# Eight column pairs by eleven block products instead of seven, the residual kept in memory meanwhile, and fixed places for the preparation steps of the last part

## The chip, the cores and the metric

The kernel runs on one core of one Trainium2 chip. The metric is device time in microseconds. TensorE does the matmuls (weights are loaded beside them), VectorE and ScalarE the elementwise work, GpSimd issues transfers and does a little arithmetic, SyncE (SP) issues most loads. Each engine takes its instructions in the order in which they were issued to it.

## The reference

One step of a two-layer model on 384 rows: 256 of a prompt and 8 × 16 of samples, so three blocks of 128 rows. D = 2048, C = 4096, everything float32. Layer 0 (attention of two kinds) comes first and is not touched by the change. Layer 1 and the end are:

```python
h = rmsnorm(x, norm1_g)                       # x: residual, 384 x 2048
p = einsum('bsd,dn->bsn', h, w_in1)           # w_in1: 2048 x 12288
u, v, z = p[..., :C], layernorm(p[..., C:2*C], ln_g, ln_b), p[..., 2*C:]
w = where(causal, w_sp, 0)                    # 16 groups of 256 columns, chunks of 128 rows
mixed = einsum('gts,bnsgc->bntgc', w, v) + b_sp
x = x + einsum('bsn,nd->bsd', u * mixed * silu(z), w_out1)     # w_out1: 4096 x 2048
y = rmsnorm(x, final_g)
```

The normalised v rows of the samples are an output too.

## The kernel before, in words

**Three products for each matmul.** Every float32 operand is split into a high part (a rounded copy, by ScalarE) and a low part (what is left, by VectorE), and each product is made as high·high, high·low and low·high (`products`, lines 100 to 102). A weight block of 128 × 512 is loaded by SP (`raw`), copied by ScalarE (`whi`, line 84) and subtracted by VectorE (`wlo`, line 86). `dense_nat` does this for a column of 512: for each of `KT` = 16 row blocks of the weights, nine matmuls, three for each block of rows of the activations, so 144 for a column with 2048 input rows. After every two row blocks it may call a step of other work, a hook (`between`).

**A pair of columns by fewer products.** Two columns can be made together by `seven`, which forms sums of the weights' and of the activations' quarters as fast matrix multiplication does: the first two blocks of 128 rows take seven block products for eight, the third takes its four as usual. That makes eleven block products of 24 matmuls, 264, where two columns by `dense_nat` take 288. `seven` has three phases of four steps each, `singles`, `chain` and `pair`; a step loads one to four wide blocks (128 × 1024, line 932, tile `sraw`), may add or subtract them on VectorE (`add`, line 958), splits them (`split2`, lines 90 and 91, tiles `shi` and `slo`) and multiplies (`stream`, lines 945 to 947, into banks `a`). The sums of the activations are made once, by `token_sums`, inside the second dense column (`sumh`, `suml`). `wide()` gives the wide buffers, five of them; `shi` and `slo` have three each.

**Order in the middle of layer 1.** Two columns of v come from `dense_nat`, the other six from three pairs (`v_pair`). Then z column c and u column c come together from one `zu_pair`, for c below `NP`; the columns from `NP` to 6 are made by `eight`, as in `dense_nat`, and their single row blocks are laid in between the steps of the pairs by the numbers in `mix`: how many ordinary row blocks stand ahead of each of the four steps of `chain` and of `pair`. `run` prepares each step (loads, sums, splits) before the products of the step ahead of it are issued. z is passed through Silu and multiplied with u and `rstd`, and the result, the gate, goes to memory (`gd`); v goes to memory too (`vd`).

**The last part.** Column 7 of z and of u come from two `dense_nat` calls; z's Silu is line 1239, u's multiplication line 1242. Their hooks, and those of `out1`, carry `prepare(c)` for c = 0 to 7: load v and the gate and the spatial weights (small loads on GpSimd's queue, line 1173), normalise v, split it, do the spatial matmuls (lines 1209 to 1211) and multiply the gate by the result (line 1213); then `turn` the gate (VectorE transposes 32 × 32 squares, line 132, and sixteen GpSimd transfers move them to their places in `gTt`, line 135) and split the turned gate into two slots (lines 1221 and 1222). `hooked(c)` runs c's steps and then c + 1's, one step a hook. `out1(k0, 8)` multiplies eight row blocks of `w_out1` with the gates of two values of c, for each of four output columns, and adds the result to the residual `h1`, which lies in four slots on the chip (line 1166). It is called for row blocks 0, 8 and 16; a shorter last part closes the sums and normalises. TensorE's dense results go to banks `d`; a column takes three, and there are four.

Of the kernel before, what the change touches and what calls it, by code (L numbers as in the profile page):

```python
# [15 lines left out]
P = 128  # L16
DM = 2048
KT = DM // P
NT = 3
# [13 lines left out]
def f32(ap):  # L33
    return ap.bitcast(F32)
# [3 lines left out]
def tile_hybrid_step(  # L38
# [828 lines left out]
    with ExitStack() as l1:  # L867
# [8 lines left out]
        with ExitStack() as lv:  # L876
# [25 lines left out]
                    gated(z, tb, o[tb])  # L902
                G.dma_start(gd[c], z)

            sums_hi, sums_lo = [], []

            def wide():
                return vp.tile([P, 2, 512], F32, tag="sraw", bufs=5, name=nm("sraw"))

            def token_sums(q):  # L910

                hi, lo = h1c[q]
                full, t = wide().rearrange("p j (h t) -> p j h t", h=2), wide().rearrange("p j (h t) -> p (j h) t", h=2).rearrange("p i (j t) -> p i j t", j=2)
                V.tensor_tensor(out=full.rearrange("p j h t -> p (j h) t"), in0=f32(hi[:, :, :2 * P]), in1=f32(lo[:, :, :2 * P]), op=ALU.add)
                a11, a12, a21, a22 = (full[:, :, h, tb * P:tb * P + P] for tb in range(2) for h in range(2))
                for i, (x, y) in enumerate(((a21, a22), (a11, t[:, 0]), (a21, a11), (a12, t[:, 1]))):
                    V.tensor_tensor(out=t[:, i], in0=x, in1=y, op=ALU.subtract)
                th, tl = (vp.tile([P, 4, 2, P], F32R, tag=tag, bufs=4, name=nm(tag)) for tag in ("sumh", "suml"))
                split(th, tl, t)
                sums_hi.append(th)  # L920
                sums_lo.append(tl)

            def row(tb, half):
                return lambda k: [x[2 * k + half][:, tb * P:(tb + 1) * P] for x in (hh_, hl_)]

            def tsum(i):
                return lambda k: [x[k // 2][:, i, k % 2, :] for x in (sums_hi, sums_lo)]

            def load2(u, half, c0):

# [2 lines left out]
                return raw  # L933

            def split2(raw):
                hi, lo = (vp.tile([P, 2 * WPITCH], F32R, tag=tag, bufs=3, name=nm(tag))[:, :1024].rearrange("p (j c) -> p j c", j=2) for tag in ("shi", "slo"))
                split(hi, lo, raw)
                return hi, lo

# [144 lines left out]
            for make, c in [(v_pair, c) for c in (2, 4, 6)] + [(zu_pair, c) for c in range(NP)]:  # L1084
                p = []

                def part(i, make=make, c=c, p=p):
                    def f(u):
                        if not p:
                            p.extend(make(c))  # L1090
                        return p[i][0](u) if u is not None else p[i][1]()
                    return f

                def closing(i, part=part):
                    f = part(i)
# [145 lines left out]
        for tb in range(NT):  # L1241
            V.scalar_tensor_tensor(out=z7[:, tb, :], in0=o[tb], scalar=rstd[:, tb:tb + 1], in1=z7[:, tb, :], op0=ALU.mult, op1=ALU.mult)
        G.dma_start(gd[7], z7)
        for k0 in (0, 8, 16):
            if k0 == 16:
                for j in range(2):
# [121 lines left out]
```

## Time and profile before

| | |
|---|---|
| time, median of 3 runs | 1789.45 us (1788.18 to 1797.57) |
| profiled execution: its time / its span | 1793.24 us / 1791.5 us |
| mean granted TensorE clock | 0.993 |
| layer 0 and the two dense columns of v | 0 to 780 us |
| pairs of v | 780 to 1046 us |
| pairs of z and u, with the ordinary row blocks among them | 1046 to 1425.8 us |
| u column 7 and the start of the last part ("the seam") | 1425.8 to 1500 us |
| three calls of `out1` | 1500 to 1760 us |

A row of a stage lists busy time of each engine in it. The rows of the trace give the start, the duration, the engine, the line of the kernel, the operation and its tiles; brackets hold the idle time of that engine just before, and what ended it. Names of tiles stand without their numbers there.

### The profile page before, as it was taken

To read this page: it belongs to the slowest core of one execution; us is meant where nothing else is said; L and a number is where in the kernel's file an instruction comes from. 1 tells how busy PE (TensorE), PEld (TensorE's weight loads), DVE (VectorE), ACT (ScalarE), POOL (GpSimd) and SP (SyncE) were. 2 spreads that over 40 slices of the span, in tenths; PEclk is the share of its full clock that TensorE was granted. 3 is DMA by queue.
4 is the path that set the end of the run, shared out by engine and by line. 5 is a ranking of instruction groups with operands and counts; after the bars stand their busy time and mean duration, and the time that the engine had idled before them with its cause. 6 is when DMAs were issued, how large, how long until landed. Compare 5 with 4: busy or idle time off the path is not lost. (4 is left out here: it accounts for less than half of the span.)

```text
span 1791.5 us, 24294 instructions
## 1 busy us (share of the span) xinstructions
PE 1748.9 (98%) x8395; PEld 1443.9 (81%) x8395; DVE 1203.1 (67%) x1784; ACT 787.5 (44%) x1273; POOL 407.2 (23%) x621
## 2 busy tenths in 40 slices
PE   9999999999999999999999999999999969999998
PEld 8987888888888888888888887787777758877887
DVE  6347475457457455677697877777777767787766
ACT  5435353345337344444454435344444334334334
POOL 6426543223221110100200000000000154455220
PEclk9999999999999999999999999999999989999999
DMA  8789989778868876677777777777776677677653
GB/s 226 195 220 199 278 214 236 221 183 226 232 177 219 252 178 168 176 266 233 249 255 264 235 258 222 232 251 238 224 224 222 200 215 235 201 207 219 190 146 116
DMA packets 218028, 389.83 MB, mean 218 GB/s; under 512 B 24024, under 2 KB 62480, under 8 KB 217904
## 3 DMA queue, kind: packets, MB, share of 16 engines
q1 hardware_dynamic: 156368, 284.09, 52.9%
q0 software_dynamic: 30704, 88.05, 19.0%
q10 hardware_dynamic: 30832, 16.13, 3.1%
q8 instruction: 66, 1.08, 0.3%
q14 instruction: 58, 0.48, 0.1%
HBM read 339.87 MB, written 42.00 MB: 213 GB/s over the span
## 5 line engine op out<-in xcount | busy, mean ns | idle before, releaser
L101 PE MATMUL d<-wlo,slot 128*128 128x512 f32 x1677 | 652.2, 390 | 0.0
L102 PE MATMUL d<-whi,slot 128*128 128x512 f32 x1677 | 650.7, 390 | 0.0
L100 PE MATMUL d<-whi,slot 128*128 128x512 f32 x1677 | 608.4, 391 | 15.6 <-ACT slot L1239 15.6
L86 DVE TENSOR_TENSOR wlo<-raw,whi 128x512 fp32r<-128x512 f32 x546 | 374.7, 696 | 313.0 <-ACT whi L84 311.0
L84 ACT ACTIVATE whi<-raw 128x512 fp32r<-128x512 f32 x546 | 342.3, 630 | 525.9 <-PE d L102 448.1
L100 PEld LDWEIGHTS d<-whi,slot 128*128 128x128 f32 x1677 | 315.3, 188 | 84.1 <-ACT slot L1239 16.1
L102 PEld LDWEIGHTS d<-whi,slot 128*128 128x128 f32 x1677 | 315.3, 188 | 66.0
L101 PEld LDWEIGHTS d<-wlo,slot 128*128 128x128 f32 x1677 | 315.4, 188 | 65.0 <-DVE wlo L86 0.2
L90 ACT ACTIVATE shi<-sraw 128x1024 fp32r<-128x1024 f32 x196 | 208.0, 1061 | 272.4 <-PE a L947 228.5
L91 DVE TENSOR_TENSOR slo<-sraw,shi 128x1024 fp32r<-128x1024 f32 x196 | 236.4, 1218 | 36.8 <-ACT shi L90 35.7
L958 DVE TENSOR_TENSOR sraw<-sraw,sraw 128x1024 f32<-128x1024 f32 x112 | 136.9, 1222 | 110.8 <-DMA sraw<-in_w_in_dram 104.0
L946 PE MATMUL a<-slo,slot 128*128 128x512 f32 x392 | 153.2, 391 | 3.3 <-DVE slo L91 3.2
L947 PE MATMUL a<-shi,slot 128*128 128x512 f32 x392 | 152.6, 389 | 0.0
L945 PE MATMUL a<-shi,slot 128*128 128x512 f32 x392 | 147.1, 390 | 0.0
L135 POOL DMA_DIRECT2D gTt<-trn x128 | 78.3, 619 | 97.1 <-ACT whi L84 69.7
L946 PE MATMUL a<-slo,sumh 128*128 128x512 f32 x224 | 89.1, 398 | 8.3 <-DVE slo L91 8.2
L946 PEld LDWEIGHTS a<-slo,slot 128*128 128x128 f32 x392 | 73.7, 188 | 20.6 <-DVE slo L91 5.4
L945 PE MATMUL a<-shi,sumh 128*128 128x512 f32 x224 | 87.9, 392 | 2.2 <-DVE slot L958 2.2
L947 PE MATMUL a<-shi,suml 128*128 128x512 f32 x224 | 88.0, 393 | 0.0
L945 PEld LDWEIGHTS a<-shi,slot 128*128 128x128 f32 x392 | 73.7, 188 | 15.4
L947 PEld LDWEIGHTS a<-shi,slot 128*128 128x128 f32 x392 | 73.7, 188 | 15.2
L464 POOL DMA_DIRECT2D slot<-d x48 | 44.1, 926 | 128.2 <-DVE wlo L86 52.7
(307 smaller groups left out, 1704.6 us busy)
## 6 DMA issues: line engine op xcount, KB each, us to landing
sraw<-in_w_in_dram SPq DMA_DIRECT2D x224, 512.0 KB, 4.6
raw<-in_w_in_dram SPq DMA_DIRECT2D x416, 256.0 KB, 4.4
raw<-in_w_out_dram SPq DMA_DIRECT2D x175, 256.0 KB, 4.1
slot<-d POOLq DMA_DIRECT2D x48, 192.0 KB, 6.2
d<-slot ACTq DMA_DIRECT2D x24, 256.0 KB, 4.2
vd<-slot POOLq DMA_DIRECT2D x8, 768.0 KB, 6.3
gd<-slot POOLq DMA_DIRECT2D x8, 768.0 KB, 6.1
v<-vd POOLq DMA_DIRECT2D x8, 768.0 KB, 7.0
```

Source lines behind the costliest of these rows:

```text
L84: highs.append(S.activation(hi, raw, AF.Copy).ins)
L86: splits.append(V.tensor_tensor(out=lo, in0=raw, in1=f32(hi), op=ALU.subtract).ins)
L90: S.activation(hi_out, src, AF.Copy)
L91: V.tensor_tensor(out=lo_out, in0=src, in1=f32(hi_out), op=ALU.subtract)
L100: PE.matmul(o, lhsT=his[k][:, t], rhs=hi[:, 0, :], start=(k == first), stop=False)
L101: PE.matmul(o, lhsT=his[k][:, t], rhs=lo[:, 0, :], start=False, stop=False)
L102: mm = PE.matmul(o, lhsT=los[k][:, t], rhs=hi[:, 0, :], start=False, stop=(k == last))
L135: G.dma_start(dst[32 * j:32 * j + 32, :, 32 * a:32 * a + 32], trn[32 * a:32 * a + 32, :, 32 * j:32 * j + 32])
L945: PE.matmul(o, lhsT=xh, rhs=hi[:, j, :], start=(u + j == 0), stop=False)
L946: PE.matmul(o, lhsT=xh, rhs=lo[:, j, :], start=False, stop=False)
L947: PE.matmul(o, lhsT=xl, rhs=hi[:, j, :], start=False, stop=(u == 3 and j == 1))
L958: V.tensor_tensor(out=out, in0=x, in1=y, op=op)
```

## The change

Five pairs of z and u are made by `seven` instead of four (`NP`), so four ordinary columns are left instead of six, and `mix` lays in fewer of their row blocks. `wide()` has eight buffers, `shi` and `slo` four. The high parts of the token sums, and the low parts of two of the four, go into shared slots, which are free because the residual is not kept in its four slots during this time: it is loaded back from `h1d`, where it lies in memory anyway, by twelve GpSimd transfers after u's column 7. In the last part the steps of `prepare` get fixed places (`first_plan`, `later_plan`): each hook runs the steps that the plan lists for it, for c and c + 1 side by side. `prepare` loads its two normalising vectors (`lg`, now two buffers) ahead of the gate, and has one more step, between the turn and the two split operations.

```diff
-                return vp.tile([P, 2, 512], F32, tag="sraw", bufs=5, name=nm("sraw"))
+                return vp.tile([P, 2, 512], F32, tag="sraw", bufs=8, name=nm("sraw"))
...
-                th, tl = (vp.tile([P, 4, 2, P], F32R, tag=tag, bufs=4, name=nm(tag)) for tag in ("sumh", "suml"))
-                split(th, tl, t)
...
+                x = slot().rearrange("p (i j t) -> p i j t", j=2, t=P)
+                th = x[:, :4]
+                spare.append(x[:, 4:])
+                S.activation(th, t, AF.Copy)
+                if q in (1, 3):
+                    tl, n = spare[-2:], 2
+                else:
+                    tl, n = [vp.tile([P, 4, 2, P], F32R, tag="suml", bufs=2, name=nm("suml"))], 4
...
-                hi, lo = (vp.tile([P, 2 * WPITCH], F32R, tag=tag, bufs=3, ...
+                hi, lo = (vp.tile([P, 2 * WPITCH], F32R, tag=tag, bufs=4, ...
...
-            NP = 4
+            NP = 5
...
-                for i, mix in ((1, (3, 3, 3, 3)), (2, (1, 0, 1, 0))):
+                for i, mix in ((1, (2, 2, 2, 1)), (2, (1, 0, 0, 0))):
...
-            lg = lp.tile([P, 2, 512], F32, tag="lg", bufs=1, name=nm("lg"))
+            lg = lp.tile([P, 2, 512], F32, tag="lg", name=nm("lg"))
...
             load_v(c)
+            norm = normalise(c)
+            next(norm)
             gate = lp.tile([P, NT, 512], F32, tag="gate", name=nm("gate"))
             G.dma_start(gate, gd[c])
             wTs = [spatial_weights(2 * c + i) for i in range(2)]
-            yield from normalise(c)
+            yield
+            for _ in norm:
+                yield
             yield
             vh, vl = split_values(c)
...
             turn(gate, gT, lp.tile([P, NT * 4, P], F32, tag="trn", bufs=1, name=nm("trn")))
+            yield
...
-        def both(c):
-            yield from prepare(c)
-            yield
-            yield from prepare(c + 1)
-
-        def hooked(c, n=16):
-            it = both(c)
-            return [lambda: next(it, None) and None for _ in range(n)]
-
-        h = hooked(0)
+        preps = [prepare(c) for c in range(8)]
+
+        def hooked(plan):
+            def at(i):
+                def f():
+                    for step in plan:
+                        for c, when in step:
+                            if when == i:
+                                next(preps[c], None)
+                return f
+            return [at(i) for i in range(16)]
+
+        def times(c, *whens):
+            return [(c, i) for i in whens]
+
+        first_plan = [times(0, 0, 4, 5, 6, 7, 8, 9, 12), times(1, 2, 7, 8, 9, 10, 11, 12, 15), times(2, 13)]
+
+        def later_plan(c):
+            return [times(c, 0, 1, 2, 3, 5, 6, 10), times(c + 1, 1, 4, 7, 8, 9, 11, 12, 15)] + ([times(c + 2, 13)] if c < 6 else [])
+
+        h = hooked(first_plan)
...
         G.dma_start(gd[7], z7)
+        for c in range(4):
+            h1[c] = slot(F32).rearrange("p (t c) -> p t c", t=NT)
+            for tb in range(NT):
+                G.dma_start(h1[c][:, tb, :]..., h1d[c, :, tb * P:(tb + 1) * P, :]...)
...
-            out1(k0, 8, hooked(k0 // 4 + 2))
+            out1(k0, 8, hooked(later_plan(k0 // 4 + 2)))
```

The instructions of the two dense columns of v and of all that comes before them keep their order, but for the token sums. Behind them three places are shown, with what the engine is issued before the change and after it. Numbers tell tiles of one name apart; they differ between the two kernels.

First piece, ScalarE, around the end of z's column 7: `whi` are the copies of the weight blocks, `wTh` those of the spatial weights, the Silu of z is line 1239 before and 1265 after, and the copies of the first turned gate are line 1221 before and 1235 after. Before:

```order
L84 ACTIVATE whi_13002<-raw_13000 128x512
L84 ACTIVATE whi_13008<-raw_13006 128x512
L90 ACTIVATE wTh_12910<-wT_12907 128x256
L90 ACTIVATE wTh_12923<-wT_12920 128x256
L1221 ACTIVATE slot_12857<-gTt_12838 128x384 x4
L1239 ACTIVATE slot_12586<-d_12587,rstd 128x512
L1239 ACTIVATE slot_12586<-d_12588,rstd 128x512
L1239 ACTIVATE slot_12586<-d_12589,rstd 128x512
L84 ACTIVATE whi_13035<-raw_13033 128x512
L84 ACTIVATE whi_13041<-raw_13039 128x512
```

The same place after:

```order
L84 ACTIVATE whi_12943<-raw_12941 128x512
L90 ACTIVATE wTh_12693<-wT_12690 128x256
L1265 ACTIVATE slot_12580<-d_12581,rstd 128x512
L1265 ACTIVATE slot_12580<-d_12582,rstd 128x512
L84 ACTIVATE whi_12989<-raw_12987 128x512
L1265 ACTIVATE slot_12580<-d_12583,rstd 128x512
L84 ACTIVATE whi_12995<-raw_12993 128x512
L90 ACTIVATE vh_13017<-v_12677 128x512 x3
L90 ACTIVATE wTh_12706<-wT_12703 128x256
L84 ACTIVATE whi_13027<-raw_13025 128x512
```

The copies of the turned gate have moved from ahead of the Silu to behind it, a whole column later: they now stand behind the first two weight copies of the first output column.

Second piece, VectorE, around the turn of the second gate (c = 1): line 132 is the transpose, `wlo` the splits of the weight blocks, lines 1174 and 1183 build spatial weights, 1236 is the low part of the first turned gate, 1268 the gating of u's column 7. Before:

```order
L86 TENSOR_TENSOR wlo_13190<-raw_13186,whi_13188 128x512
L132 STREAM_TRANSPOSE trn_13152<-gate_12899 128x1536
L86 TENSOR_TENSOR wlo_13214<-raw_13210,whi_13212 128x512
L86 TENSOR_TENSOR wlo_13220<-raw_13216,whi_13218 128x512
L86 TENSOR_TENSOR wlo_13244<-raw_13240,whi_13242 128x512
L86 TENSOR_TENSOR wlo_13250<-raw_13246,whi_13248 128x512
L1174 TENSOR_TENSOR wr_13281<-w_7070,btri 128x128
```

After:

```order
L86 TENSOR_TENSOR wlo_13326<-raw_13322,whi_13324 128x512
L132 STREAM_TRANSPOSE trn_13116<-gate_12682 128x1536
L86 TENSOR_TENSOR wlo_13332<-raw_13328,whi_13330 128x512
L1137 SCALAR_TENSOR_TENSOR v_13164<-v_13164,mvr,lg_13166 128x512
L1183 TENSOR_TENSOR wr_13361<-w_7070,btri 128x128
L1183 TENSOR_TENSOR wr_13374<-w_7070,btri 128x128
L1236 TENSOR_TENSOR slot_13106<-gTt_12965,slot_13105 128x384 x3
L1268 SCALAR_TENSOR_TENSOR slot_12580<-d_12910,rstd,slot_12580 128x512
L1236 TENSOR_TENSOR slot_13106<-gTt_12965,slot_13105 128x384
L1268 SCALAR_TENSOR_TENSOR slot_12580<-d_12911,rstd,slot_12580 128x512
L1138 SCALAR_TENSOR_TENSOR v_13164<-v_13164,rsv,lg_13166 128x512
L1268 SCALAR_TENSOR_TENSOR slot_12580<-d_12912,rstd,slot_12580 128x512
```

Before, six splits of u's column 7 (four of them shown) stood behind the turn and ahead of u's gating; now the turn stands between the first two splits of the first output column (`wlo_13326` and `wlo_13332`), and the four low parts of the first gate stand between it and the end of u's gating.

Third piece, GpSimd's queue from that turn of the second gate on: line 135 moves the turned squares, 1243 or 1269 stores the gate of column 7, 1130 or 1139 stores an output, 1273 loads the residual. Before:

```order
L135 DMA gTt_13151<-trn_13152 32x12x32 x16
L1196 DMA gate_13592<-gd_7082 128x1536
L1173 DMA wr_13594<-in_w_sp_dram 32x4x32 x4
L1173 DMA wr_13607<-in_w_sp_dram 32x4x32 x4
L1243 DMA gd_7086<-slot_12586 128x1536
L1130 DMA out_dram<-v_13277 128x512
L1123 DMA lg_13620<-in_sgu_ln_g_dram 128x512
L1124 DMA lg_13620<-in_sgu_ln_b_dram 128x512
L1117 DMA v_13975<-vd_7075 128x1536
L135 DMA gTt_13531<-trn_13532 32x12x32 x16
```

After:

```order
L135 DMA gTt_13115<-trn_13116 32x12x32 x16
L1269 DMA gd_7086<-slot_12580 128x1536
L1139 DMA out_dram<-v_13164 128x512
L1132 DMA lg_13881<-in_sgu_ln_g_dram 128x512
L1133 DMA lg_13881<-in_sgu_ln_b_dram 128x512
L1182 DMA wr_13886<-in_w_sp_dram 32x4x32 x4
L1182 DMA wr_13899<-in_w_sp_dram 32x4x32 x4
L1273 DMA slot_13301<-h1d 128x4x128 x3
L1273 DMA slot_13305<-h1d 128x4x128 x3
L1273 DMA slot_13309<-h1d 128x4x128 x3
L1273 DMA slot_13313<-h1d 128x4x128 x3
L1126 DMA v_13879<-vd_7075 128x1536
```

The twelve loads of the residual stand behind the sixteen transfers of the second gate's turn and twelve more transfers, where before there was no load of it at all.

More of the change, by code (lines that the diff above doesn't have):

```diff
@@ L903, in evict_u @@
                 G.dma_start(gd[c], z)
-            sums_hi, sums_lo = [], []
+            sums, spare = [], []
             def wide():
-                return vp.tile([P, 2, 512], F32, tag="sraw", bufs=5, name=nm("sraw"))
+                return vp.tile([P, 2, 512], F32, tag="sraw", bufs=8, name=nm("sraw"))
             def token_sums(q):
@@ L917, in token_sums @@
                     V.tensor_tensor(out=t[:, i], in0=x, in1=y, op=ALU.subtract)
-                th, tl = (vp.tile([P, 4, 2, P], F32R, tag=tag, bufs=4, name=nm(tag)) for tag in ("sumh", "suml"))
-                split(th, tl, t)
-                sums_hi.append(th)
-                sums_lo.append(tl)
+                x = slot().rearrange("p (i j t) -> p i j t", j=2, t=P)
[6 more added lines that the diff above has]
+                    tl, n = [vp.tile([P, 4, 2, P], F32R, tag="suml", bufs=2, name=nm("suml"))], 4
+                lows = []
+                for i, x in enumerate(tl):
+                    V.tensor_tensor(out=x, in0=t[:, i * n:i * n + n], in1=f32(th[:, i * n:i * n + n]), op=ALU.subtract)
+                    lows += [x[:, j] for j in range(n)]
+                sums.append(([th[:, i] for i in range(4)], lows))
             def row(tb, half):
@@ L926, in tsum @@
             def tsum(i):
-                return lambda k: [x[k // 2][:, i, k % 2, :] for x in (sums_hi, sums_lo)]
+                return lambda k: [x[i][:, k % 2, :] for x in sums[k // 2]]
             def load2(u, half, c0):
@@ L935, in split2 @@
             def split2(raw):
-                hi, lo = (vp.tile([P, 2 * WPITCH], F32R, tag=tag, bufs=3, name=nm(tag))[:, :1024].rearrange("p (j c) -> p j c", j=2) for tag in ("shi", "slo"))
+                hi, lo = (vp.tile([P, 2 * WPITCH], F32R, tag=tag, bufs=4, name=nm(tag))[:, :1024].rearrange("p (j c) -> p j c", j=2) for tag in ("shi", "slo"))
                 split(hi, lo, raw)
@@ L1243, in tile_hybrid_step @@
         G.dma_start(gd[7], z7)
+        for c in range(4):
+            h1[c] = slot(F32).rearrange("p (t c) -> p t c", t=NT)
+            for tb in range(NT):
+                G.dma_start(h1[c][:, tb, :].rearrange("p (k d) -> p k d", k=4), h1d[c, :, tb * P:(tb + 1) * P, :].rearrange("k t d -> t k d"))
         for k0 in (0, 8, 16):
```

## The prediction

> **What bounds the kernel now.** First the page's busy line, then one table of busy time by stage: its columns are the stretch, its length, then busy time (instructions) of TensorE, weight loads, VectorE, ScalarE, GpSimd, then the granted clock, the DMA share, GB/s.
>
> ```profile
> span 1791.5 us, 24294 instructions
> PE 1748.9 (98%) x8395; PEld 1443.9 (81%) x8395; DVE 1203.1 (67%) x1784; ACT 787.5 (44%) x1273; POOL 407.2 (23%) x621
> ```
> ```profile
> 0.00:780.00 780.00, 778.88 (x4111) 647.29 (x4112) 447.14 (x796) 357.64 (x675) 246.13 (x341) 1.00 0.81 212
> 780.00:1046.00 266.00, 263.40 (x1160) 217.19 (x1159) 207.23 (x225) 120.88 (x141) 13.49 (x23) 1.00 0.77 248
> 1046.00:1425.80 379.80, 368.53 (x1596) 299.06 (x1596) 282.40 (x303) 167.10 (x195) 7.64 (x17) 1.00 0.72 232
> 1425.80:1500.00 74.20, 58.57 (x255) 48.09 (x254) 45.68 (x82) 24.82 (x44) 38.90 (x68) 0.88 0.68 210
> 1500.00:1760.00 260.00, 256.44 (x1145) 211.83 (x1144) 201.96 (x336) 105.65 (x189) 99.02 (x170) 1.00 0.69 198
> ```
>
> TensorE bounds every stage. Time can only come from fewer matmuls or from its waits. Third, what a matmul costs: the timeline of TensorE, where the modelled 0.39 us of a row overlaps the next row, so one must read the starts.
>
> ```profile
> 1423.11 0.39 PE L946 MATMUL a<-slo,slot 128*128 128x512 f32 x1
> ...
> 1432.63 0.39 PE L102 MATMUL d<-whi,slot 128*128 128x512 f32 x1
> ...
> 1469.81 0.80 PE L100 MATMUL d<-whi,slot 128*128 128x512 f32 x1 [15.63 <-ACT slot L1239]
> 1470.40 0.63 PE L101 MATMUL d<-wlo,slot 128*128 128x512 f32 x1
> ...
> 1473.39 0.63 PE L102 MATMUL d<-whi,slot 128*128 128x512 f32 x1
> ```
>
> From 1423.11 to 1432.63 there are 42 steps: 0.2267 us a matmul, not the 0.39 of its row. By that step the pair stage lost 266 − 1160 × 0.2267 = 3.0 us in its three v pairs and 379.8 − 1596 × 0.2267 = 18.0 us in its four z/u pairs: 1.0 and 4.5 a pair, 21 in all. The seam to the last part lost 15.6 us in one wait, and about 2.0 more since the rows from 1470.40 to 1473.39 are 0.43 apart, half speed. From 1500 to 1760 the two waits of row L1209 below make 3.5.
>
> ```profile
> PE d L100 <- ACT slot L1239: 15.6, 1, 15.6
> PE a L946 <- DVE slo L91: 11.5, 12, 2.2
> PE a L1209 <- ACT vh L90: 3.5, 2, 1.8
> ```
>
> So there are about 42 us of lost time: 21 in the pair stage, 21 behind it. The 780 us ahead are issued as before and stay.
>
> **Part 1: one more pair by eleven products.** It replaces 288 matmuls by 264: 24 × 0.2267 = **−5.4 us**, since TensorE is the bound. What it asks of VectorE:
>
> ```profile
> L91 DVE TENSOR_TENSOR slo<-sraw,shi 128x1024 fp32r<-128x1024 f32 x196 | 236.4, 1218 | 36.8 <-ACT shi L90 35.7
> L958 DVE TENSOR_TENSOR sraw<-sraw,sraw 128x1024 f32<-128x1024 f32 x112 | 136.9, 1222 | 110.8 <-DMA sraw<-in_w_in_dram 104.0
> L86 DVE TENSOR_TENSOR wlo<-raw,whi 128x512 fp32r<-128x512 f32 x546 | 374.7, 696 | 313.0 <-ACT whi L84 311.0
> ```
> ```profile
> 1131.93 1.22 DVE L958 TENSOR_TENSOR sraw<-sraw,sraw 128x1024 f32<-128x1024 f32 x1 [3.43 <-DMA sraw<-in_w_in_dram]
> 1133.08 3.49 DVE L91 TENSOR_TENSOR slo<-sraw,shi 128x1024 fp32r<-128x1024 f32 x3
> ```
>
> Three wide splits in a row take 3.49, so 1.14 each and 0.08 once. A pair has 28 wide splits and 16 wide sums, 44 × 1.14 = 50; about 14 narrow closing operations at 0.6 (0.696 less the same overlap), 8.6; and its share of ordinary row blocks at 0.6, before 14, now 8. That is 67 us before in (264 + 126) × 0.2267 = 88.4, 76% (the z/u row has 282.4 of 379.8, 74%), and 63.5 after in 336 × 0.2267 = 76.2: **83%**. VectorE stays below TensorE, with less slack. DMA: 32 wide loads of 0.524 MB and 8 narrow ones of 0.262 per pair are 18.9 MB in 76.2 us, 248 GB/s, and with the stores (0.8 or 1.6 MB) 258 to 269. The first 100 us of the stage carry nearly that with no lost time:
>
> ```profile
> 780.00:880.00 100.00, 100.00 (x443) 82.84 (x442) 78.07 (x88) 45.29 (x54) 5.65 (x9) 1.00 0.77 248
> ```
>
> At 0.77 for 248 GB/s, 269 would be a share of 0.84. It fits.
>
> **Part 2: eight wide buffers for five, four split buffers for three.** Who makes VectorE late in the stage? Its waits, and the DMA queue's own:
>
> ```profile
> DVE sraw L958 <- DMA sraw<-in_w_in_dram: 104.0, 60, 4.1
> ```
> ```profile
> SPq L932 <- DVE slo L91: 342.3, 190, 5.5
> ```
> ```profile
> sraw<-in_w_in_dram SPq DMA_DIRECT2D x224, 512.0 KB, 4.6
> ```
>
> The load of a wide block waits on the queue until a split frees one of five buffers (190 times), then takes 4.6 us to land; VectorE waits for it in order (60 times) and holds the three ready splits of row 1133.08 behind it, and TensorE waits for these (L946). A chain step takes four wide blocks, so five buffers reach one load ahead and eight a whole step, 24 × 0.2267 + 2 × 2.04 = 9.5 us, twice the 4.6. I expect most of these waits to go. Bounds for the stage's lost time: nothing, as in its first 100 us, and 4.5 a z/u pair and 1.0 a v pair as now, 5 × 4.5 + 3 × 1.0 = 25.5; below that VectorE's load, priced under the rivals. I take 1.25 a pair, near the v pairs' row, because they have the looser supply that the buffers give: 10 us for 21, **−11**.
>
> Moving the four sums into shared slots adds no matmul and two half-size operations, in a dense block where TensorE loses nothing (row 0 to 780): nothing, and if that cover were gone 2 × 0.1.
>
> **Part 3: places in the last part.** The seam:
>
> ```profile
> 1453.74 1.77 DVE L132 STREAM_TRANSPOSE trn<-gate 128x1536 f32<-128x1536 f32 x1
> 1456.15 9.75 POOL L135 DMA_DIRECT2D gTt<-trn  x16 [3.55 <-DVE wT L1177]
> 1467.42 1.76 ACT L1221 ACTIVATE slot<-gTt 128x384 fp32r<-128x384 f32 x4 [8.92 <-DMA gTt<-trn]
> 1467.98 1.96 DVE L1222 TENSOR_TENSOR slot<-gTt,slot 128x384 fp32r<-128x384 f32 x4 [7.66 <-ACT slot L1221]
> 1469.09 1.82 ACT L1239 ACTIVATE slot<-d,rstd 128x512 f32<-128x512 f32 x3
> ```
>
> ScalarE stands 8.9 us before the gate's copies, for 16 issues that take GpSimd 9.75, and the Silu that frees TensorE's banks is queued behind them. In the new order (first piece) that Silu has only splits ahead of it and the copies come a whole block later: the 15.6 + 2.0 go. The two L1209 waits go too, since a hook now lies between split and products: 3.5.
>
> What is late next? The second gate, column c = 1 (second and third piece). Its turn has slipped behind the first split of the next block. Let E be the end of the u block. That split can start when the fourth row block before it is through, 21 matmuls before E, about −4. Then VectorE has the turn 1.77, four copies 1.96, and five operations at 0.7 or less to pass: 7 us, so the last copy of c = 0 is at E + 3. Only then may GpSimd write the one gTt: 9.75, and 1.5 to the copies as in the rows above (1465.9 to 1467.42), first copy at E + 14.8. TensorE wants it four row blocks and twelve products in, 36 × 0.2267 + 2.1 = E + 10.3: a wait of 4.5.
>
> The residual comes back behind that turn on the same queue: store, one output, two constants, eight small loads, then twelve new loads.
>
> ```profile
> 1425.85 4.41 POOL L1173 DMA_DIRECT2D wr<-in_w_sp_dram  x8 [3.65 <-PE a L947]
> ```
> ```profile
> slot<-h1d POOLq DMA_DIRECT2D x4, 192.0 KB, 7.2
> blk<-h1d POOLq DMA_DIRECT2D x12, 192.0 KB, 9.0
> h1d<-slot ACTq DMA_DIRECT2D x12, 256.0 KB, 2.6
> ```
>
> Eight take 4.41, 0.55 each: E + 3 + 9.75 + 12 × 0.55 = E + 19.4, issue and landing (7.2; the nearest rows give 2.6 to 9.0) to E + 27, first sum at E + 28. TensorE closes the first output column at E + 18.4 and has one spare bank, 12 matmuls, to E + 21.1: 7 us late in all, the 4.5 included. Half speed after it adds up to 2. I take **9** for 21, **−12**; bounds 2 (loads landing like the fastest row and VectorE ahead) and 14 (9.0, and every gap at half speed). The later loads have 16 us each and are hidden by that; the end of the kernel is unchanged.
>
> On half speed, another row: a wait of 2.15 us was already followed by 0.43 steps.
>
> ```profile
> 1319.52 0.50 PE L946 MATMUL a<-slo,sumh 128*128 128x512 f32 x1 [2.15 <-DVE slo L91]
> ...
> 1323.23 0.63 PE L947 MATMUL a<-shi,suml 128*128 128x512 f32 x1
> ```
>
> The Trainium skill, page "TensorE: Matmul & The Clock Gate", section "What's actually happening", has the clock halved only after an idle window of about 3.4 us. By it the pieces above cost no half speed where each stays under 3.4, and the sum would be 2 us lower; the row of 2.15 us says otherwise, and the sum above goes by the row.
>
> **Sum.** The profiled execution took 1793.24 us (span 1791.5). −5.4 − 11 − 12 = −28.4 gives 1764.8. That execution lies 3.8 above the median of the runs, 1789.45; taken off, 1761.
>
> **Rivals.** *The buffers bring nothing* (the bound is DMA speed, not depth; for it, 0.84 of share; against it, the first 100 us): lost time 25.5 for 21, 1761 + 15.5 = 1777. *The last part gives its gain back*, by the second gate and the residual as reckoned, but larger: 21 lost again, 1761 + 12 = 1773. *VectorE becomes the bound, slower than before*: it waits in order for matrices and DMA, and in the z/u pairs of before it did 76%, as reckoned. Held to that, a pair takes 63.5 / 0.76 = 83.6, 7.4 over its 76.2; eight pairs lose 59 for 21. Without part 2's gain and with the last part's that is 1761 − 10 + 59 = 1810, and it is slower than before once VectorE cannot pass about 78%, 63.5 / 0.78 = 81.4, where eight pairs lose 42. Against it: the z/u row's idle quarter has a cause that part 2 removes, and row 780 to 880 stands at 78% with TensorE unstarved. *GpSimd's issue slows under a denser VectorE*: if each issue waited for one narrow operation, 0.7 more on 28 issues, the residual would come 20 us later: 1781. The rows speak against it, 128 issues between 615 and 644 ns in the stretch where VectorE is busy 202 of 260 us:
>
> ```profile
> L135 POOL DMA_DIRECT2D gTt<-trn x128: 615/617/644, 1456.1 to 1714.5; - x128
> ```
>
> The Trainium skill, page "SBUF — State Buffer", section "A bandwidth-pool intuition that's wrong (but worth ruling out)", has such an issue grow from about 620 to 3100 ns beside a VectorE copy; 16 at that price would be 50 us, and no run before shows it.
>
> **How the numbers follow.** The forecast 0.62 (its own range 1750 to 1771); buffers bring nothing 0.13; last part's gain gone 0.09; VectorE bound 0.08; slower issue 0.03; the second and third together, 1789, 0.05. A measurement of this kernel can tell 0.5% from no change, 9 us: faster under 1780.5, slower over 1798.4. The first three are faster, 0.84, less 0.01 for their tails. VectorE's case is slower, 0.07 of its 0.08. The rest, 0.10, is no change. The range reaches down to no loss in the pairs (−10) and 2 in the last part (−7), with some of both, and up past 1777: 1747 to 1782.
>
> **What would show it.** Right: TensorE has 24 matmuls fewer; DVE's wait for sraw loads falls from 104 to under 30 us and PE's for slo with it; no wait on the Silu of z7; near the first output column one wait of TensorE for the gate's copies and one for banks behind the sum with h1. Wrong: DVE over 90% busy with TensorE still waiting for slo; SP's waits gone but loads landing in 8 us instead of 4.6; a wait of 15 us on h1 or gTt.

## The result, and the profile after

The changed kernel takes 1780.06 us, median of 6 runs (1775.91 to 1781.56), where the kernel before took 1790.34 in the 6 runs beside them (1788.18 to 1797.57). The ratio is 0.9932, 95% interval 0.9910 to 0.9955: a gain of 10 us where 28 were forecast. The profiled execution took 1779.61 us. Its busy line, and the page's own rows for the operations that the prediction followed (line 967 was 958, L135 the turn's transfers):

```profile
span 1777.9 us, 24259 instructions
PE 1744.8 (98%) x8371; PEld 1442.2 (81%) x8371; DVE 1234.1 (69%) x1808; ACT 800.2 (45%) x1271; POOL 418.7 (24%) x633
L967 DVE TENSOR_TENSOR sraw<-sraw,sraw 128x1024 f32<-128x1024 f32 x128 | 156.4, 1222 | 71.2 <-DMA sraw<-in_w_in_dram 70.6
L135 POOL DMA_DIRECT2D gTt<-trn x128 | 78.4, 619 | 73.8 <-ACT whi L84 31.3
sraw<-in_w_in_dram SPq DMA_DIRECT2D x256, 512.0 KB, 4.8
```

The 24 matmuls are gone (8395 to 8371). VectorE waits 70.6 us for wide loads, not the "under 30" of the prediction, and a load takes 4.8 us for 4.6. TensorE's waits:

```profile
PE a L954 <- DVE slot L967: 9.5, 5, 2.6
PE d L100 <- ACT slot L1235: 7.0, 2, 4.1
PE a L955 <- DVE slo L91: 2.3, 3, 1.7
PE a L954 <- ACT slot L894: 1.4, 1, 1.4
PE d L100 <- DVE slot L1175: 1.0, 1, 1.0
```

The wait on z's Silu is gone, and the waits for `slo` fell from 11.5 us to 2.3. But another wait has grown to the top: products of the pair stage (L954) held by a VectorE operation that is no split. `slot L967` is a closing operation, which reads a bank and so frees it. In the kernel before this wait was 2.2 us:

```profile
PE a L945 <- DVE slot L958: 2.2, 5, 1.3
```

Three stages, in the columns of the prediction's table, of before and of after (up to the first product of a pair, up to the last one, and up to the last matmul):

```profile
0.00:780.10 780.10, 778.98 (x4112) 647.35 (x4113) 447.24 (x796) 357.74 (x675) 246.13 (x341) 1.00 0.81 212
780.10:1425.40 645.30, 631.43 (x2753) 515.84 (x2752) 489.16 (x526) 287.88 (x335) 21.13 (x40) 1.00 0.74 239
1425.40:1782.80 357.40, 338.21 (x1533) 280.59 (x1532) 264.25 (x455) 140.28 (x260) 139.28 (x239) 0.98 0.66 194
```
```profile
0.00:781.50 781.50, 780.02 (x4111) 646.84 (x4112) 445.82 (x798) 358.06 (x676) 245.46 (x341) 1.00 0.80 212
781.50:1411.80 630.30, 617.07 (x2698) 507.89 (x2697) 522.15 (x545) 297.95 (x328) 28.39 (x48) 0.99 0.79 257
1411.80:1769.10 357.30, 347.44 (x1564) 287.40 (x1562) 263.71 (x459) 142.54 (x264) 144.21 (x244) 0.99 0.68 204
```

By steps of 0.2267 us the pair stage loses 645.3 − 2753 × 0.2267 = 21 us before and 630.3 − 2698 × 0.2267 = 18.7 after. The last row holds shorter matmuls too, so its loss, here and below, is what TensorE's steps over 0.26 us have beyond 0.227, added up from the trace; by that measure it is 22.3 before and 14.9 after, and the pair stage 20.9 and 18.7. So the way to the last matmul is 13.7 shorter: 5.4 from the matmuls, 2.2 from the pair stage, 7.4 from the last part, less 1.2 in the first 780 us.

**Where the pair stage loses now.** The timeline of TensorE, then of VectorE, at the end of one chain phase of the changed kernel:

```profile
1231.32 0.68 PE L954 MATMUL a<-shi,slot 128*128 128x512 f32 x1 [2.20 <-DVE slot L967]
1231.80 0.63 PE L955 MATMUL a<-slo,slot 128*128 128x512 f32 x1
1232.22 0.63 PE L956 MATMUL a<-shi,suml 128*128 128x512 f32 x1
```
```profile
1217.60 1.23 DVE L967 TENSOR_TENSOR sraw<-sraw,sraw 128x1024 f32<-128x1024 f32 x1 [1.10 <-DMA sraw<-in_w_in_dram]
...
1220.93 1.22 DVE L967 TENSOR_TENSOR sraw<-sraw,sraw 128x1024 f32<-128x1024 f32 x1 [1.51 <-DMA sraw<-in_w_in_dram]
1222.08 3.49 DVE L91 TENSOR_TENSOR slo<-sraw,shi 128x1024 fp32r<-128x1024 f32 x3
1225.48 0.69 DVE L86 TENSOR_TENSOR wlo<-raw,whi 128x512 fp32r<-128x512 f32 x1
1229.35 1.23 DVE L967 TENSOR_TENSOR sraw<-sraw,sraw 128x1024 f32<-128x1024 f32 x1 [3.18 <-DMA sraw<-in_w_in_dram]
1230.49 0.68 DVE L967 TENSOR_TENSOR slot<-a,slot 128x512 f32<-128x512 f32 x1
```

The rows that write `sraw` are weight sums of the phase that comes next, `pair`. With eight wide buffers the scheduler puts all four of them ahead of the closing of `chain` (the first here, at 1211.26, is not shown; in the first pair it is three). The kernel before has two ahead and two behind, as in this pair, where the closing is the run of `slot` rows from 1212.53 on:

```profile
1210.79 1.23 DVE L958 TENSOR_TENSOR sraw<-sraw,sraw 128x1024 f32<-128x1024 f32 x1 [1.12 <-DMA sraw<-in_w_in_dram]
1211.93 0.68 DVE L86 TENSOR_TENSOR wlo<-raw,whi 128x512 fp32r<-128x512 f32 x1
1212.53 0.68 DVE L958 TENSOR_TENSOR slot<-a,slot 128x512 f32<-128x512 f32 x1
...
1218.33 1.23 DVE L958 TENSOR_TENSOR sraw<-sraw,sraw 128x1024 f32<-128x1024 f32 x1
```

In the changed kernel the fourth sum, at 1229.35, waits 3.18 us for its load, the closing at 1230.49 stands behind it, and TensorE stands without a bank until 1231.32, then runs seven steps at half speed (0.43 apart). One such wait, of 1.5 to 2.7 us by the steps, comes in six of the eight pairs, and in three of these a product waits for a split ahead of it as well. That VectorE holds a ready operation behind one that waits agrees with the Trainium skill, page "PSUM — Partial Sum Buffer", section "Engine vs sequencer instructions", which calls its queue strictly first in, first out.

### The profile page after: what moved, and what is told of

It is laid out like the page before. It is cut to its first block, busy times and chain, and to the rows that moved or that the text cites. A ratio compares the mean times of both kernels' runs of the same rounds, so it can differ in the third digit from the quotient of the medians.

```text
span 1777.9 us, 24259 instructions
## 1 busy us (share of the span) xinstructions
PE 1744.8 (98%) x8371; PEld 1442.2 (81%) x8371; DVE 1234.1 (69%) x1808; ACT 800.2 (45%) x1271; POOL 418.7 (24%) x633
## 5 line engine op out<-in xcount | busy, mean ns | idle before, releaser
L101 PE MATMUL d<-wlo,slot 128*128 128x512 f32 x1581 | 616.9, 391 | 0.0
L102 PE MATMUL d<-whi,slot 128*128 128x512 f32 x1581 | 613.9, 390 | 0.0
L100 PE MATMUL d<-whi,slot 128*128 128x512 f32 x1581 | 571.1, 392 | 8.6 <-ACT slot L1235 7.0
L100 PEld LDWEIGHTS d<-whi,slot 128*128 128x128 f32 x1581 | 297.8, 188 | 75.0 <-ACT slot L1235 7.4
L90 ACT ACTIVATE shi<-sraw 128x1024 fp32r<-128x1024 f32 x224 | 237.1, 1061 | 268.0 <-PE a L956 247.5
L102 PEld LDWEIGHTS d<-whi,slot 128*128 128x128 f32 x1581 | 297.2, 188 | 62.7 <-DVE slot L1236 0.5
L91 DVE TENSOR_TENSOR slo<-sraw,shi 128x1024 fp32r<-128x1024 f32 x224 | 269.6, 1219 | 35.5 <-ACT shi L90 33.5
L954 PE MATMUL a<-shi,slot 128*128 128x512 f32 x704 | 269.3, 392 | 10.9 <-DVE slot L967 9.5
L955 PE MATMUL a<-slo,slot 128*128 128x512 f32 x704 | 275.2, 391 | 2.3 <-DVE slo L91 2.3
L956 PE MATMUL a<-shi,slot 128*128 128x512 f32 x576 | 223.6, 389 | 0.0
L967 DVE TENSOR_TENSOR sraw<-sraw,sraw 128x1024 f32<-128x1024 f32 x128 | 156.4, 1222 | 71.2 <-DMA sraw<-in_w_in_dram 70.6
L954 PEld LDWEIGHTS a<-shi,slot 128*128 128x128 f32 x704 | 133.0, 189 | 40.9 <-issue 11.5
L955 PEld LDWEIGHTS a<-slo,slot 128*128 128x128 f32 x704 | 132.7, 189 | 31.0 <-DVE slo L91 3.6
L956 PEld LDWEIGHTS a<-shi,slot 128*128 128x128 f32 x576 | 108.3, 188 | 22.4
L135 POOL DMA_DIRECT2D gTt<-trn x128 | 78.4, 619 | 73.8 <-ACT whi L84 31.3
L967 DVE TENSOR_TENSOR slot<-a,slot 128x512 f32<-128x512 f32 x72 | 48.0, 684 | 4.1 <-PE a L956 4.1
```

The costliest lines, as they stand in the source:

```text
L90: S.activation(hi_out, src, AF.Copy)
L91: V.tensor_tensor(out=lo_out, in0=src, in1=f32(hi_out), op=ALU.subtract)
L100: PE.matmul(o, lhsT=his[k][:, t], rhs=hi[:, 0, :], start=(k == first), stop=False)
L101: PE.matmul(o, lhsT=his[k][:, t], rhs=lo[:, 0, :], start=False, stop=False)
L102: mm = PE.matmul(o, lhsT=los[k][:, t], rhs=hi[:, 0, :], start=False, stop=(k == last))
L135: G.dma_start(dst[32 * j:32 * j + 32, :, 32 * a:32 * a + 32], trn[32 * a:32 * a + 32, :, 32 * j:32 * j + 32])
```

## The experiments

All ratios are against runs of the kernel before that were made beside the kernel's own on the same chip, so kernels of different rows are better compared by ratio than by time. Lost time is by the measure above, of the profiled execution.

| kernel | ratio to before, 95% interval | pair stage loses, us | last part loses, us |
|---|---|---|---|
| before | 1 | 20.9 | 22.3 |
| changed | 0.9932 (0.9910 to 0.9955) | 18.7 | 14.9 |
| two sums late | 0.9772 (0.9753 to 0.9792) | 0.0 | 6.8 |
| three sums late | 0.9777 (0.9757 to 0.9797) | 0.5 | 6.9 |
| five buffers | 1.0199 (1.0176 to 1.0222) | 42.1 | 39.8 |
| four pairs | 0.9799 (0.9779 to 0.9820) | 0.0 | 5.5 |
| four pairs, thin | 0.9867 (0.9850 to 0.9885) | 15.1 | 3.0 |
| cover first | 0.9820 (0.9804 to 0.9837) | 6.7 | 3.2 |
| old last part | 0.9881 (0.9867 to 0.9895) | 0.1 | 24.3 |
| steps earlier | 0.9785 (0.9769 to 0.9800) | 0.1 | 7.3 |
| copies ahead | 0.9917 (0.9896 to 0.9938) | 21.0 | 13.2 |
| both cures | 0.9835 (0.9818 to 0.9852) | 0.0 | 16.0 |
| both cures, copies ahead | 0.9827 (0.9810 to 0.9845) | 0.7 | 13.5 |
| steps earlier still | 0.9786 (0.9769 to 0.9802) | 0.0 | 6.3 |

**Two sums late, three sums late.**

```diff
-                    add(b12, b22, b12)
+                    with ExitStack() as late:
+                        if u > 1:                        # three sums late: u > 0
+                            late.enter_context(tc.issue_after(m["closed"].ins))   # last closing operation of chain
+                        add(b12, b22, b12)
```

Not shown are the lines that keep the last closing operation in `m["closed"]`.

> The changed kernel, with the third and fourth weight sum of the pair phase issued on VectorE only after the closing operations of the chain phase (the first two stay where the scheduler puts them). Theory, held closing: with eight buffers all four sums stand ahead of the closing, the last of them waits for its load, and TensorE waits for banks; without that the lost time of the pair stage falls from 18.7 us to about 7 and the time from 1780 to about 1769 (ratio to before about 0.988), with TensorE's waits at the bank of a closing (9.5 us) under 4. Rival, supply: the loads land too late whatever the order, VectorE only waits elsewhere: 1780, within 2. Rival, VectorE's load (83 per cent): nothing moves, 1780.

> The changed kernel, with the second, third and fourth sum of the pair phase after the closing of the chain phase. Held closing: as with two sums moved or 1 to 2 us better, 1767 to 1770; worse than that by up to 5 if the second sum is then late for its own split. Supply or VectorE's load: 1780.

Measured 1753.02 and 1754.45 us. VectorE at the same place of the kernel with two sums late, and its pair stage:

```profile
1218.48 0.69 DVE L967 TENSOR_TENSOR slot<-a,slot 128x512 f32<-128x512 f32 x1 [0.35 <-PE a L956]
...
1223.05 0.67 DVE L967 TENSOR_TENSOR slot<-slot,a 128x512 f32<-128x512 f32 x1
1223.64 2.35 DVE L967 TENSOR_TENSOR sraw<-sraw,sraw 128x1024 f32<-128x1024 f32 x2
```
```profile
782.40:1395.30 612.90, 612.90 (x2705) 507.51 (x2704) 521.97 (x544) 297.82 (x329) 27.21 (x49) 1.00 0.82 266
```

The closing now waits for TensorE's last product (L956), not the other way round, and the two sums behind it find their loads landed. TensorE is busy for all of the 612.9 us. The same row shows VectorE busy 522 of 613 (85%) and the DMA at a share of 0.82 with 266 GB/s: neither VectorE's load nor the supply was the limit, and both rivals fall. VectorE still waits 42.1 us for wide loads in this kernel, more than the "under 30" of the prediction, and in the pair stage this costs TensorE nothing. The gain is more than twice what was expected, because the whole loss went and the last part, which the scheduler lays out anew, lost 8 less.

**Five buffers.** `sraw` 5 and `shi`, `slo` 3 in the changed kernel.

> The changed kernel with five wide buffers and three split buffers, as before the change. Forecast's account (buffers are worth 4.5 us a z/u pair where they are short): the pair stage loses 5 x 4.5 + 3 = 25 us for 18.7, the time is 1787. Rival, the buffers bring nothing by themselves: 1780, within 2. Rival, more buffers do harm, since they let the sums run ahead of the closing: below 1777.

1829.13 us, 2% slower than before. VectorE again waits 106.4 us for wide loads and TensorE 19.1 for `slo`:

```profile
PE a L955 <- DVE slo L91: 19.1, 21, 2.2
PE d L100 <- ACT slot L1235: 18.1, 3, 11.1
```

This is 42 more than expected. By the ratios the buffers are worth about 48 us at this mix of pairs and ordinary blocks, half of it in the pair stage; "the buffers bring nothing" is dead, and so is "more buffers do harm". It is not by four sums ahead of the closing that this kernel loses: in its trace, two at most stand ahead of the first closing operation in every pair, as before the change. So it is with more buffers that the scheduler lets the others run ahead. What its last part loses was not followed further.

**Four pairs, and four pairs thin.** `NP = 4` with the numbers of before (3 3 3 3, 1 0 1 0), and with the changed kernel's (2 2 2 1, 1 0 0 0); the order of the sums left to the scheduler.

> The changed kernel with four pairs of z and u and the old numbers of ordinary row blocks between the steps (3 3 3 3, 1 0 1 0): part 1 undone. Held closing: 24 more matmuls are 5.4 us, seven such places for eight give 2 back: 1783. Rival, the closing lost its cover since only two ordinary row blocks for three stand ahead of the chain phase: the waits for banks go, about 13 us, and the time is 1772.

> The kernel with four pairs of z and u (1758 us with 3 3 3 3 and 1 0 1 0 ordinary row blocks in front of the steps), with the thinner numbers of the changed kernel instead (2 2 2 1 and 1 0 0 0); the ordinary row blocks left over run behind the last pair. The same matmuls. Theory, held closing through thin cover: the fourth sum waits for its load and holds the closing in each of seven pairs, 16 to 19 us are lost again: 1774 to 1777. Rival, it is the fifth pair itself (its loads, its VectorE work) and not the numbers: 1758, within 3.

1758.15 and 1767.88 us; the first is below both times that were expected of it. The two have the same matmuls and eight buffers each. Their pair stages and, for the thin one, TensorE's first wait:

```profile
783.10:1402.00 618.90, 618.90 (x2732) 512.45 (x2732) 487.71 (x523) 288.83 (x331) 29.06 (x49) 1.00 0.77 250
```
```profile
781.10:1331.70 550.60, 540.42 (x2363) 445.01 (x2362) 455.81 (x475) 260.65 (x288) 26.24 (x45) 0.99 0.80 259
```
```profile
PE a L954 <- DVE slot L967: 10.0, 6, 2.4
```

With three ordinary row blocks ahead of the chain's steps there is no loss, though there too four sums stand ahead of the closing and the fourth waits, here 2.38 us:

```profile
1200.32 1.23 DVE L967 TENSOR_TENSOR sraw<-sraw,sraw 128x1024 f32<-128x1024 f32 x1 [2.38 <-DMA sraw<-in_w_in_dram]
1201.46 1.29 DVE L86 TENSOR_TENSOR wlo<-raw,whi 128x512 fp32r<-128x512 f32 x2
1202.66 0.68 DVE L967 TENSOR_TENSOR slot<-a,slot 128x512 f32<-128x512 f32 x1
```

It is over before the banks are wanted. So two things make the loss together: sums that run ahead of the closing, and too little ordinary work to let them wait. Take away the first (two sums late) or the second (four pairs) and the pair stage loses nothing. It is the numbers, not the fifth pair. The thin kernel lost 10 in time, 12 by the ratios, for 16 to 19 expected: the pair stage gave the 15.1, the last part took 2.5 less.

**Cover first.** The eight ordinary row blocks a pair as (3, 2, 1, 0) and (2, 0, 0, 0).

> The changed kernel (1780 us) with its eight ordinary row blocks a pair laid out as 3 2 1 0 ahead of the chain's steps and 2 0 0 0 ahead of the pair phase, the order of the sums left to the scheduler. Theory, held closing through thin cover: 18 matmuls instead of 9 (4.1 us for 2.0) stand between the chain's last product and the next banks, the waits of 1.6 to 2.7 us and the half speed behind them go: the pair stage loses under 5 us for 18.7, about 1765. Rival, only the order on VectorE counts, the sum waits just as long: 1780, or worse by the third and fourth steps that have less cover.

1760.55 us, better than expected: the waits at closings fall from 9.5 us to 3.1. (Its profiled execution took 1756.07, lower than its other runs.) Nothing was moved on VectorE by hand, but the scheduler moved something itself: in every pair the fourth sum now stands behind the first closing operation.

```profile
1223.81 0.69 DVE L967 TENSOR_TENSOR slot<-a,slot 128x512 f32<-128x512 f32 x1
...
1227.30 1.23 DVE L967 TENSOR_TENSOR sraw<-sraw,sraw 128x1024 f32<-128x1024 f32 x1 [1.67 <-DMA sraw<-in_w_in_dram]
```

So this run does not tell cover from order. The two kernels with four pairs do: in both, the four sums stand ahead of the closing of `chain`, but for one sum of the first pair.

**Old last part.** Two sums late, with `prepare`, `both` and `hooked` of before; the residual is still reloaded, and `lg` keeps its two buffers.

> The kernel with the two later sums behind the closing (1753 us), with the last part's plan, prepare and lg buffer use of before (c, then c + 1, one step a hook); the residual is still reloaded. Forecast's account of part 3: the wait of z's Silu, its half speed and the two waits at the split values (21 us) come back for the 7 that are lost there now: 1767 to 1770. Rival, the seam's wait was a consequence of the pair stage ending with late buffers, and the plan is worth little: 1753 to 1758.

1770.33 us, at the upper end of the range expected. The Silu's wait is back at 12.1 us, with the two at the split values, 3.5, and a wait of 2.2 for the residual. Part 3 is worth 17 us by the traces (24.3 against 6.8) and 20 by the ratios in a kernel whose pair stage is on time.

```profile
PE d L100 <- ACT slot L1251: 12.1, 1, 12.1
PE a L1221 <- ACT vh L90: 3.5, 2, 1.8
PE d L100 <- DVE slot L1178: 2.2, 2, 1.9
```

**The last part: copies ahead, steps earlier, both cures.** The changed kernel waits for the copies of the second gate, as forecast, and again for those of the fourth, which was not. TensorE, then ScalarE, at the fourth:

```profile
1572.81 0.79 PE L100 MATMUL d<-whi,slot 128*128 128x512 f32 x1 [2.89 <-ACT slot L1235]
```
```profile
1569.60 0.42 ACT L90 ACTIVATE wTh<-wT 128x256 fp32r<-128x256 f32 x1 [1.07 <-PE a L1223]
1571.91 0.42 ACT L90 ACTIVATE wTh<-wT 128x256 fp32r<-128x256 f32 x1 [1.90 <-DVE wT L1187]
1572.24 1.75 ACT L1235 ACTIVATE slot<-gTt 128x384 fp32r<-128x384 f32 x4
```

The copies stand behind both high copies of the next spatial weights, and the second of these waits for VectorE. With two sums late the scheduler puts one of the two behind the gate's copies, and TensorE waits 0.6:

```profile
1547.08 0.42 ACT L90 ACTIVATE wTh<-wT 128x256 fp32r<-128x256 f32 x1 [1.07 <-PE a L1226]
1547.41 1.75 ACT L1238 ACTIVATE slot<-gTt 128x384 fp32r<-128x384 f32 x4
```

Copies ahead: the odd gates' copies at place 14 of the plan, the next column's start at 14 behind them, and its high copies tied behind the gate's.

> The changed kernel (1780 us), in the last part alone: the copies of the odd gates stand ahead of both high copies of the next spatial weights on ScalarE (copies at place 14, the next column's start at 14 behind them). Theory: in the changed kernel the odd gates' copies stand behind both of these and wait with them for small GpSimd loads; without that the wait of 2.9 us with its half speed at the fourth gate goes and the one of 4.2 at the second shrinks to the landing of the turned gate, so the last part loses about 8 to 10 us for 14.9, the pair stage keeps its 18.7: 1773 to 1776. Rival, the transfers of the turn are what is late: 1780, within 2.

1776.47 us. The fourth gate's wait shrank to 1.3 and 0.7, but the second gate's grew from 4.1 to 8.7, since the next spatial matmuls no longer stand in front of it: the last part lost 13.2 for 8 to 10 expected. The second gate's copies come as late as in the changed kernel, 15.8 us for 15.5 after u's first gating operation, and ScalarE itself now waits 6.9 us for the gate's transfers (1.7 there). So at this gate it was the transfers that were late, as the rival said. The interval of its ratio overlaps the changed kernel's, so this run decides little.

Steps earlier (two sums late): the plan's steps one place earlier, the first gate's copies at 11 for 12, the second's turn and copies at 11 and 14 for 12 and 15. Steps earlier still: 10, and 10 and 13.

> The kernel with the two later sums behind the closing (1753 us), with the steps of both gates one hook earlier from the normalisation on (first_plan 0: 0 3 4 5 6 7 8 11, 1: 2 6 7 8 9 10 11 14; later_plan c: 0 1 2 3 4 5 9, c + 1: 1 3 6 7 8 9 10 13). If the second gate's turn is late as the forecast says, its wait (2.7 and 0.4 half speed) and part of the residual's wait (1.2) go: 1749 to 1751. If the small loads of the spatial weights hold ScalarE's copies and not the turn, it is no better: 1753 or more.

> The kernel with the two later sums behind the closing (1753 us), with the first gate's copies two places earlier (10 for 12), and the second gate's turn and copies at 10 and 13 for 12 and 15; in the calls of out1 the same steps two or three places earlier. Theory: the second gate's sixteen transfers can only leave behind the first gate's copies, since there is one gTt; with these about 8 us earlier than in that kernel TensorE no longer waits for the second gate (2.7 us and 0.4) nor for the residual behind it (1.2): the last part loses 2 to 4 us for 6.75, 1749 to 1751. Rival, the transfers leave earlier but the steps now collide with the normalisation, whose loads are not there yet: 1753 or more.

1752.80 and 1753.41 us: no gain over 1753.02, both expectations of 1749 to 1751 missed. The transfers do leave earlier, and "1753 or more" of both rivals fits. The second gate's copies come 10.0 us after u's first gating operation in both, for 12.8 with two sums late; but now TensorE waits up to 2.0 for the low parts behind them.

Both cures (two sums late and cover first), and the same with copies ahead:

> Both cures of the pair stage together: two later sums behind the closing, and 3 2 1 0 / 2 0 0 0 ordinary row blocks. Nothing is left to gain in the pair stage (0.0 lost with the sums moved alone), the last part may lose 3.2 as with the cover alone for 6.75: 1749 to 1753. If the third and fourth step of the chain, now with less cover, wait for their splits: 1755 to 1758.

> Both cures of the pair stage, and the odd gates' copies ahead of the next spatial weights: pair stage 0 to 1 lost, last part 2 to 4: 1747 to 1750. If the next spatial weights are then late for their own matmuls: 1752 to 1756.

1762.69 and 1760.84 us, both worse than expected. Nothing is lost in the pair stage, but 16.0 and 13.5 in the last part. In the first of these both high copies stand ahead of the fourth gate's copies again, and its wait is again 2.9; the second gate's is 6.6. What sets the second gate's wait, 0.6 to 8.7 us over the kernels with the new plan and eight buffers in which it shows, is not settled beyond this: its sixteen transfers leave only behind the first gate's copies, since there is one `gTt`, and in these kernels the scheduler puts those copies 2.9 to 11.0 us ahead of the first gating of u's column 7. The best kernel of the study is two sums late: 1753.02 us, 2.3% under the kernel before and 1.6% under the changed one (0.9772 / 0.9932).

## Why the prediction was wrong

Of the some 19 us between the forecast of 1761 and the measured 1780, 8.8 lie in part 2, 4.6 in part 3, 1.2 in the first 780 us and 3.8 in the last subtraction.

- **Part 1, −5.4 from the matmuls: right as a price, wrong as an edit.** Two sums late against four pairs, run side by side and both without loss in the pair stage, is 1753.02 against 1758.15: −5.1. But the step "It replaces 288 matmuls by 264 … since TensorE is the bound" took the thinner numbers of ordinary row blocks for free. Those blocks give TensorE work while a closing frees the banks. With four pairs, thinning them costs 10 to 12 us; in the changed kernel, by the ratios, five pairs thin stand 0.0133 × 1791 = 24 us above four pairs with the old numbers.
- **Part 2, −11: 2.2 came.** The step that failed is "five buffers reach one load ahead and eight a whole step … I expect most of these waits to go", and with it the 1.25 us a pair, where 2.3 came (18.7 over eight pairs). The buffers do supply more, 48 us' worth against five. But what stands behind a waiting sum was asked of the old order alone (the three splits of row 1133.08). The new order on VectorE was read at the last part and not here, where eight buffers let two more sums run ahead of the closing of `chain`. TensorE's wait moved from the splits to the closings.
- **Part 3, −12: 7.4 came.** The reckoned pieces held, one of them with luck: the second gate's copies came 15.5 us after E (here u's first gating operation; reckoned 14.8), by transfers that started earlier (1.5 after E for 3) and a longer way from their last issue to the copies (4.1 for 1.5). The terms of the 14.8 add up to 14.3, which would have made the wait 4.0. The wait was 4.1 for 4.5, half speed behind it 2.1 for 2, and the residual cost 1.0 for 2.5. Missed were the fourth gate's 2.9 with 1.7 of half speed behind it, and 2.7 in small waits, most of them at the spatial matmuls. That the later loads "are hidden" looked at the loads and not at ScalarE's queue.
- **The 3.8 us that the profiled execution lay above the median** were taken off the sum. The profiled executions differ by 13.6, the medians by 10.3, and the changed kernel's profile (1779.61) lies at its median: if that is no accident of one execution each, part of the excess sat in what the change removed. The runs do not show more than that.
- **The first 780 us, nothing:** they grew by 1.2, of which 0.6 is a new wait at 703.8, beside the token sums. The other kernels of the study, with the same work there, lost 5.4 to 9.9 where before lost 4.6, so this is within what one execution shows.
- **The rivals.** The measured 1780 lies inside the widened 1747 to 1782, but above the forecast's own 1750 to 1771, and the end that it lies at was drawn for rivals. Two named times came near by causes that did not happen. "GpSimd's issue slows" gave 1781, but an issue took 619 ns in the row of 128 above, as before; "the buffers bring nothing" gave 1777, and five buffers refute it. VectorE as the bound is refuted at 85% busy with no wait of TensorE (two sums late). The cause of the pair stage's loss was none of the rivals.

## What to carry to other kernels

More buffers also let a scheduler hoist work, and in an in-order queue a hoisted operation that waits for its load holds everything behind it: look for the operation that frees the scarce thing (here a bank), and keep what waits for memory behind it. Work that looks like filler may be the cover of such a hand-over; when it is thinned, price the hand-over, and read the order of the new program at every stage that the sum counts on, not only where the old trace had its largest wait.

## What the hardware showed

TensorE's half speed comes in whole windows. In the traces' record of the granted clock, from the pair stage to the last matmul, it stands at 0.50 for 3.41 us at a time or a multiple of it, and within one execution all these times lie on one grid of steps of 3.413 us, whose borders do not follow the waits. Here are two waits of the changed kernel, the one that ended at 1231.32 and another that ended at 1152.12, each as the window of the grid that holds it and the window behind it, in the columns of the tables by stage:

```profile
1228.00:1231.42 3.42, 1.22 (x6) 0.71 (x6) 2.07 (x3) 1.52 (x3) 0.00 (x0) 1.00 0.66 225
1231.42:1234.83 3.41, 3.41 (x9) 2.64 (x10) 3.41 (x5) 0.00 (x0) 0.00 (x0) 0.50 0.37 98
1149.50:1152.91 3.41, 1.71 (x9) 1.10 (x8) 2.76 (x3) 0.63 (x1) 0.00 (x0) 1.00 0.37 140
1152.91:1156.32 3.41, 3.41 (x16) 2.80 (x15) 3.41 (x6) 0.71 (x1) 0.00 (x0) 1.00 0.55 154
```

The first wait emptied its window for 2.36 us beyond the usual steps of 0.227, and the next window ran at half speed; the second emptied its own for 1.87, and nothing followed. Over all 14 profiles, from 790 us to the last matmul, every one of the 22 windows at full speed that were empty for 2.0 us or more was followed by half speed. Of the seven between 1.89 and 2.0 two were, and of those with less none was. So a wait counts by what of it falls into one window: of 20 steps of TensorE that lasted 2.0 to 2.9 us beyond the usual 0.227, 12 were followed by half speed, and 8, which a border of the grid cut in two, by none. All of the 11 longer ones (2.9 to 15.8) were followed by it, and of the shorter ones, from 1.0 us on, two. It costs 1.1 to 2.9 us, hardly more after a long wait than after a short one. The Trainium skill, page "TensorE: Matmul & The Clock Gate", section "What's actually happening", names an idle window of about 3.4 us and calls the window free-running. The grid of 3.413 us agrees with it; that about 2 us without matmuls in one window suffice does not agree with a whole idle window, and the measurement decides.
